# Gate and up projection: a fourth seven-product K pair per column chunk, and one weight sum made by an adding transfer

## The chip, the cores and the metric

The kernel runs on one core of one Trainium2 chip. The metric is the device time of one execution in microseconds. Before the change it was 2225.26 us, the median of three runs (2225.0 to 2226.5). A profiled execution is one further run, taken by the hardware profiler.

## The reference

Two layers of a residual trunk work on 256 tokens of width 2048 in float32. Only the feed-forward half of a layer bears on this case:

```python
def swiglu(h, w_gate, w_up, w_down):
    return (jax.nn.silu(h @ w_gate) * (h @ w_up)) @ w_down

for l in range(DEPTH):                       # DEPTH = 2
    h = rms_norm(x, pre_mix_norm[l])
    x = x + rms_norm(hybrid_mixer(h, l, ...), post_mix_norm[l])   # w_in 2048 x 6144, attention, w_o 2048 x 2048
    h = rms_norm(x, pre_ffn_norm[l])
    x = x + rms_norm(swiglu(h, w_gate[l], w_up[l], w_down[l]), post_ffn_norm[l])
```

w_gate and w_up are 2048 x 5632, w_down is 5632 x 2048. All weights are float32, and the result keeps float32's accuracy: every product is made of three matmuls on rounded halves of its operands.

## The kernel before, in words

**Weights as a stream.** All weight matrices are cut into pieces of 256 rows (a "K pair": two K tiles of 128) by 512 columns. `queue_pair` (L93) lists them in the order of use. `fetch` (L135) loads piece i with a DMA on SyncE's queue (L139) into a tile `raw`, of which there are four, each 128 x 2 x 512 float32 (512 KB). `feed` (L166) turns a piece into two tiles: `hi`, its rounded copy (ScalarE, L176), and `lo`, the rest (VectorE, L178); there are six of each. `weights` (L186) feeds four pieces ahead of the use (`LOOKAHEAD`). A load waits for a free `raw` tile, so for the end of an earlier piece's `lo`; a `hi` waits until TensorE has read an earlier piece's `hi`.

**Gate and up.** The 5632 columns are 11 chunks of 512 (loop at L827). A chunk has 8 K pairs, and for each K pair the stream holds a gate piece and then the up piece. There are two ways to multiply a K pair by the 256 tokens (two blocks of 128):

- `eight` (L810): 2 K tiles x 2 token blocks x 2 matrices are 8 products of 3 matmuls of 128x512 (L706 to L708), 24 in all. Both pieces are split as above.
- `seven` (L820): Strassen's scheme in Winograd's form over the 2 x 2 blocks (token block by K tile, K tile by gate or up), with 7 products, 21 matmuls, by `seven_products` (L723). It needs sums of token blocks (`pair_sums` and `token_sums`, made once per layer in the first chunk at the places that `FORM_AT` names) and sums of weight blocks: with g0, g1, u0, u1 for the two K tiles of the gate and up pieces, t1 = g0 + u0, t3 = u0 + u1, t2 = t1 + u1 and t4 = t2 + g1. Four of the products have no accumulator of their own in the output, so they gather in four further PSUM banks (p1, p6, p7, q5) over the chunk's seven-product pairs, and `shared_part` (L740) adds them up at the end.

`SEVEN` (L36) names the K pairs of a chunk that go by `seven`: 2, 4 and 6; the first chunk, which has its own order, has 4 and 6 (`FIRST_SEVEN`). `mixed_weights` (L144) makes the weight sums for such a pair: four additions on VectorE (L150, 128x512) from the two `raw` tiles into two tiles `T` of the pool `gu`, then the rounded copies `Th` (ScalarE, L159) and the rests `Tl` (VectorE, L161) of both, and the split of u1 alone (L154, L155).

At the end of a chunk VectorE adds up the shared parts (L744 to L747) and the results (L853 to L856) from PSUM, with ScalarE's Silu between; `flip` (L858) transposes them on TensorE (L862) during the next chunk.

**Down.** Two halves of 22 K pairs follow; six pairs of each go by seven products as well (`DOWN_SEVEN`, L40), with the same `mixed_weights`. The tiles `T`, `Th` and `Tl` then lie in a pool `sums`, which takes the space of the tokens' tiles `xF` once gate and up have read them (L868).

**Order.** A scheduler of the framework orders each engine's instructions when the program is built, and each engine then works through its queue strictly in that order. The tile pools hand a new tile the slot that is expected to come free first. The order of the loads on SyncE's queue and of the splits on VectorE's is thus fixed beforehand.

Of the kernel before, what the change touches and what calls it, by code (L numbers as in the profile page):

```python
# [17 lines left out]
P = 128  # L18
D = 2048
S = 256  # L20
L = 2
NT = S // P
KT = D // P
NH = 8
FF = 5632
CW = 512
# [16 lines left out]
LEVEL = 232  # L43


def lambda_init(layer):
    return 0.8 - 0.6 * math.exp(-0.3 * layer)


@with_exitstack  # L50
def kernel(
# [3 lines left out]
    w_in: bass.AP,  # L55
    w_o: bass.AP,
# [6 lines left out]
    w_gate: bass.AP,  # L63
    w_up: bass.AP,
    w_down: bass.AP,
    rope: bass.AP,
    x_columns: bass.AP,
    gain_columns: bass.AP,
    out: bass.AP,
# [21 lines left out]
    stream = []  # L91

    def queue_pair(w2d, kp, c):  # L93
        stream.append(
            w2d[kp * 2 * P : (kp + 1) * 2 * P, c * CW : (c + 1) * CW].rearrange("(k p) n -> p k n", p=P)
        )
        return len(stream) - 1

    plan = []
    sevens = set()  # L100
    for l in range(L):
        lay = {"in": {}, "o": {}, "gate": {}, "up": {}, "down": {}}
        chunks = []
        for g in range(2):
            chunks += [6 + g, 8 + g, 10 + g]
        for g in range(2):
            chunks += [g, 2 + g, 4 + g]
        lay["chunks"] = chunks
        for c in chunks:
            for kp in range(KT // 2):  # L110
                lay["in"][c, kp] = queue_pair(w_in[l], kp, c)
        order_o = [(c, kp) for kp in KP_O for c in (0, 1)]
        order_o += [(c, kp) for c in (2, 3) for kp in range(KT // 2)]
        lay["order_o"] = order_o
        for c, kp in order_o:
            lay["o"][c, kp] = queue_pair(w_o[l], kp, c)
        for c in range(FF // CW):
            for kp in FIRST_ORDER if c == 0 else range(KT // 2):
                lay["gate"][c, kp] = queue_pair(w_gate[l], kp, c)
                lay["up"][c, kp] = queue_pair(w_up[l], kp, c)  # L120
                if kp in (FIRST_SEVEN if c == 0 else SEVEN):
                    sevens.add(lay["up"][c, kp])
        for half in range(2):
            for kp in range(FF // P // 2):
                for c in (2 * half, 2 * half + 1):
                    lay["down"][c, kp] = queue_pair(w_down[l], kp, c)
                if kp in DOWN_SEVEN:
                    sevens.add(lay["down"][2 * half + 1, kp])
        plan.append(lay)
# [5 lines left out]
    def fetch(upto):  # L135
        while len(raws) < min(upto, len(stream)):
            i = len(raws)
            raw = wpool.tile([P, 2, CW], F32, tag="raw", bufs=4, name=f"raw{i}")
            loads.append(nc.sync.dma_start(raw, stream[i]))  # L139
            raws.append(raw)  # L140

    mix_pool = [None]

    def mixed_weights(i):  # L144

        g, u = raws[i - 1], raws[i]
        sums = [mix_pool[0].tile([P, 2, CW], F32, tag="T", bufs=2, name=f"T{i}_{j}") for j in range(2)]
        t1, t3, t2, t4 = sums[0][:, 0, :], sums[0][:, 1, :], sums[1][:, 0, :], sums[1][:, 1, :]
        for o, a, b in ((t1, g[:, 0, :], u[:, 0, :]), (t3, u[:, 0, :], u[:, 1, :]), (t2, t1, u[:, 1, :]), (t4, t2, g[:, 1, :])):
            nc.vector.tensor_tensor(out=o, in0=a, in1=b, op=ALU.add)  # L150
        parts = []
        hi = wpool.tile([P, 2, CW], F32R, tag="hi", bufs=6, name=f"hi{i}")
        lo = wpool.tile([P, 2, CW], F32R, tag="lo", bufs=6, name=f"lo{i}")
        nc.scalar.activation(hi[:, 1, :], u[:, 1, :], AF.Copy)  # L154
        nc.vector.tensor_tensor(out=lo[:, 1, :], in0=u[:, 1, :], in1=hi[:, 1, :].bitcast(F32), op=ALU.subtract)  # L155
        parts.append((hi[:, 1, :], lo[:, 1, :]))
        for j in range(2):
            th = mix_pool[0].tile([P, 2, CW], F32R, tag="Th", bufs=3, name=f"Th{i}_{j}")
            nc.scalar.activation(th, sums[j], AF.Copy)  # L159
            tl = mix_pool[0].tile([P, 2, CW], F32R, tag="Tl", bufs=3, name=f"Tl{i}_{j}")  # L160
            nc.vector.tensor_tensor(out=tl, in0=sums[j], in1=th.bitcast(F32), op=ALU.subtract)  # L161
            parts += [(th[:, k, :], tl[:, k, :]) for k in range(2)]
        b22, t1, t3, t2, t4 = parts
        return {"b22": b22, "t1": t1, "t2": t2, "t3": t3, "t4": t4}
# [50 lines left out]
    setup = tc.alloc_tile_pool(name="setup", bufs=1, side="right", reuse_waits="tile")  # L215
    idle = setup.tile([P, CW], BF16, name="idle")
# [10 lines left out]
    lams = setup.tile([P, 4, L * 64], F32, name="lams")  # L227
    negones = setup.tile([P, P], F32, name="negones")
# [6 lines left out]
    def late_constants():  # L235
# [16 lines left out]
        lprod = setup.tile([P, 2, L * 64], F32, name="lprod")  # L252
        lsum = setup.tile([P, 2, L], F32, name="lsum")
# [364 lines left out]
    def settle(pool, rs, evac):  # L618

        for t, h in ((0, 0), (0, 1), (1, 0), (1, 1)):  # L620
            load_x(t, h)
            yield 1
        late_constants()
        setup.release()
        rs += [inv_rms(t, pool, "in0") for t in range(NT)]
        yield 2
        scales(rs)
        evac()
# [121 lines left out]
    for l in range(L):  # L750
# [117 lines left out]
        mix_pool[0] = new_x_pool(f"sums{l}")  # L868
# [100 lines left out]
    "x", "w_in", "w_o", "lambda_q1", "lambda_k1", "lambda_q2", "lambda_k2",  # L969
    "post_mix_norm", "post_ffn_norm", "w_gate", "w_up", "w_down",  # L970
# [44 lines left out]
```

## Time and profile before

| what | value |
|---|---|
| median of the runs | 2225.26 us |
| the profiled execution | 2225.4 us |
| its span (first to last instruction) | 2223.6 us |
| mean granted TensorE clock | 0.998 |
| TensorE busy | 2205.6 us, 99% |
| VectorE busy | 1765.9 us, 79% |
| ScalarE busy | 1276.3 us, 57% |
| GpSimd busy | 37.4 us, 2% |
| DMA | 423.72 MB, 191 GB/s on average |

The profile names the engines PE (TensorE), PEld (its weight loads), DVE (VectorE), ACT (ScalarE), POOL (GpSimd) and SP (SyncE); SPq is SP's DMA queue. L176 is line 176 of the kernel. A row of a group reads: line, engine, operation, tiles written <- tiles read, shape, count, busy time and mean ns of one, idle time of the engine before them and what ended it. Consecutive matmuls overlap, so their spacing, not their length, is what one costs. A row of the timeline reads: start, length, engine, line, operation, tiles, and in brackets how long the engine had been idle and what released it.

### The profile page before, as it was taken

What the parts mean: (1) busy time and instruction counts of PE and PEld (TensorE: products, weight loads), DVE (VectorE), ACT (ScalarE), POOL (GpSimd) and SP (SyncE); (2) the same over time, 40 slices, a digit from 0 to 9 for tenths busy, and PEclk for the clock granted to TensorE, in tenths of its full rate; (3) what the DMA queues carried; (4) which work ended last, traced back from release to release, by engine and by line L of the source; (5) the groups of instructions that cost most, each with busy time, mean ns of one, the idle gap of its engine ahead of it and who ended that gap; (6) DMA issues with size and microseconds to landing.
All of it is one profiled execution on the core that took longest, in us unless ns stands there. A gap on an engine that the chain in (4) does not pass through costs nothing.

```text
span 2223.6 us, 28156 instructions
## 1 busy us (share of the span) xinstructions
PE 2205.6 (99%) x10117; PEld 1814.4 (82%) x10117; DVE 1765.9 (79%) x2505; ACT 1276.3 (57%) x1895; POOL 37.4 (2%) x76
## 2 busy tenths in 40 slices
PE   9999999999999999999999999999999999999998
PEld 7888888788888888888877888887888888888886
DVE  6666555899889989989876665558998898999897
ACT  6555554656555556656565455546655555566563
POOL 1100000000000000000010000000000000000000
PEclk9999999999999999999999999999999999999999
DMA  8655555466665665656555555554666565566564
GB/s 292 194 164 165 159 189 183 138 208 203 204 199 190 205 207 189 213 189 213 194 182 170 169 163 161 183 187 151 201 207 202 178 221 194 190 212 211 183 217 143
DMA packets 217996, 423.72 MB, mean 191 GB/s; under 512 B 13568, under 2 KB 14080, under 8 KB 217344
## 3 DMA queue, kind: packets, MB, share of 16 engines
q1 hardware_dynamic: 217712, 421.91, 58.8%
q8 instruction: 79, 1.29, 0.2%
q14 instruction: 61, 0.50, 0.1%
q10 hardware_dynamic: 144, 0.02, 0.0%
HBM read 419.77 MB, written 2.10 MB: 190 GB/s over the span
## 4 chain that ended last, share of the span: by engine, by line
PE 94%; ACT 2%; DVE 1%; DMA 1%; issue 0%; SPq 0%; DVEq 0%; ACTq 0%
PE c L707 10%; PE c L706 10%; PE c L708 10%; PE in L352 8%; PE in L354 8%; PE in L353 8%; PE dn L911 5%; PE dn L909 5%; PE dn L908 5%; PE o L354 2%; PE o L352 2%; PE o L353 2%; PE p L706 2%; PE p L707 2%; PE p L708 2%; ACT hi L176 1%
## 5 line engine op out<-in xcount | busy, mean ns | idle before, releaser
L178 DVE TENSOR_TENSOR lo<-raw,hi 128x1024 fp32r<-128x1024 f32 x695 | 843.9, 1224 | 309.6 <-ACT hi L176 304.4
L176 ACT ACTIVATE hi<-raw 128x1024 fp32r<-128x1024 f32 x695 | 726.9, 1056 | 497.8 <-PE in L354 164.9
L706 PE MATMUL c<-hi,xF 128*128 128x512 f32 x960 | 377.0, 394 | 1.4 <-ACT w L743 0.8
L707 PE MATMUL c<-lo,xF 128*128 128x512 f32 x960 | 373.9, 390 | 1.1 <-DVE lo L178 1.0
L708 PE MATMUL c<-hi,xF 128*128 128x512 f32 x960 | 374.0, 391 | 0.0
L159 ACT ACTIVATE Th<-T 128x1024 fp32r<-128x1024 f32 x176 | 185.7, 1056 | 141.7 <-DVE T L150 133.8
L161 DVE TENSOR_TENSOR Tl<-T,Th 128x1024 fp32r<-128x1024 f32 x176 | 214.2, 1217 | 4.4 <-ACT Th L159 3.8
L706 PEld LDWEIGHTS c<-hi,xF 128*128 128x128 f32 x960 | 180.5, 188 | 39.2 <-ACT w L743 1.2
L707 PEld LDWEIGHTS c<-lo,xF 128*128 128x128 f32 x960 | 180.6, 188 | 38.5 <-DVE lo L178 2.3
L708 PEld LDWEIGHTS c<-hi,xF 128*128 128x128 f32 x960 | 180.7, 188 | 37.8
L908 PE MATMUL dn<-hi,jh 128*128 128x512 f32 x464 | 180.7, 389 | 0.0
L909 PE MATMUL dn<-lo,jh 128*128 128x512 f32 x464 | 180.5, 389 | 0.0
L352 PE MATMUL in<-hi,xI 128*128 128x512 f32 x384 | 154.0, 401 | 0.4 <-ACT xI L293 0.4
L352 PE MATMUL in<-hi,xT 128*128 128x512 f32 x384 | 153.8, 401 | 0.5 <-ACT hi L176 0.5
L354 PE MATMUL in<-hi,xI 128*128 128x512 f32 x384 | 150.3, 391 | 0.3 <-DVE xI L298 0.3
L353 PE MATMUL in<-lo,xI 128*128 128x512 f32 x384 | 150.0, 391 | 0.5 <-DVE lo L178 0.5
L353 PE MATMUL in<-lo,xT 128*128 128x512 f32 x384 | 149.8, 390 | 0.5 <-DVE lo L178 0.5
L354 PE MATMUL in<-hi,xT 128*128 128x512 f32 x384 | 150.1, 391 | 0.0
L911 PE MATMUL dn<-hi,jl 128*128 128x512 f32 x464 | 142.8, 389 | 0.0
L150 DVE TENSOR_TENSOR T<-T,raw 128x512 f32<-128x512 f32 x176 | 120.5, 684 | 1.2
L911 PEld LDWEIGHTS dn<-hi,jl 128*128 128x128 f32 x464 | 87.1, 188 | 18.1
L908 PEld LDWEIGHTS dn<-hi,jh 128*128 128x128 f32 x464 | 87.1, 188 | 18.1
(295 smaller groups left out, 3513.8 us busy)
## 6 DMA issues: line engine op xcount, KB each, us to landing
raw<-in_w_in_dram SPq DMA_DIRECT2D x191, 512.0 KB, 3.8
raw<-in_w_gate_dram SPq DMA_DIRECT2D x176, 512.0 KB, 3.8
raw<-in_w_up_dram SPq DMA_DIRECT2D x176, 512.0 KB, 4.5
raw<-in_w_down_dram SPq DMA_DIRECT2D x176, 512.0 KB, 4.5
raw<-in_w_o_dram SPq DMA_DIRECT2D x64, 512.0 KB, 4.0
xr<-in_x_columns_dram SPq DMA_DIRECT2D x8, 256.0 KB, 6.9
x<-in_x_dram SPq DMA_DIRECT2D x4, 512.0 KB, 8.6
gpost_mix<-in_post_mix_norm_dram SPq DMA_DIRECT2D x2, 1024.0 KB, 6.9
```

Of the source, the lines that this page charges most:

```text
L161: nc.vector.tensor_tensor(out=tl, in0=sums[j], in1=th.bitcast(F32), op=ALU.subtract)
L176: nc.scalar.activation(hi, raw, AF.Copy)
L178: nc.vector.tensor_tensor(out=lo, in0=raw, in1=hi.bitcast(F32), op=ALU.subtract)
L352: nc.tensor.matmul(a, sh, hi[:, kk, :], start=first and kk == 0, stop=False)
L353: nc.tensor.matmul(a, sh, lo[:, kk, :], start=False, stop=False)
L354: nc.tensor.matmul(a, sl, hi[:, kk, :], start=False, stop=last and kk == 1)
L706: nc.tensor.matmul(a, sh, hi, start=first, stop=False)
L707: nc.tensor.matmul(a, sh, lo, start=False, stop=False)
L708: nc.tensor.matmul(a, sl, hi, start=False, stop=last)
L908: nc.tensor.matmul(accs[c, t], sh, hi[:, kk, :], start=first, stop=False)
L909: nc.tensor.matmul(accs[c, t], sh, lo[:, kk, :], start=False, stop=False)
L911: nc.tensor.matmul(accs[c, t], sl, hi[:, kk, :], start=False, stop=last)
```

## The change

1. `SEVEN` becomes (2, 4, 5, 6): in chunks 1 to 10 of each layer K pair 5 goes by seven products too. `FORM_AT` gets an entry for its token sums, made in the first chunk.
2. The sums of weight blocks are made in another way. The up piece of a seven-product pair is no longer loaded into a `raw` tile but into a tile `T` of its own (`summed`), and a second DMA, on GpSimd's queue, adds the gate piece's first half onto the tile's first half: T = (t1, u1). `fetch` issues both up to `EARLY` = 4 stream places ahead of the piece's turn. `mixed_weights` splits T as one 128x1024 tile, then makes t2 = t1 + u1 in T's second half, and t3 = t2 - g0 and t4 = t2 + g1 in place of the gate piece in its `raw` tile: three VectorE additions where there were four, and splits of 1024, 512 and 1024 columns where there were 512, 1024 and 1024. `Th` and `Tl` become two tiles of 128 x 3 x 512 instead of three of 128 x 2 x 512; there are three tiles `T` in gate and up and two in down.
3. The weights come to the device in the order of the stream, as one tensor in which each piece is a contiguous 512 KB and each of its 128 rows 4 KB (`weights_laid_out`); before, a row of a piece was two runs of 2 KB in the weight matrix.
4. To make room, the pool `setup` is gone (its tiles use `lo` and `t2` slots), the feed-forward pool has five `t2` tiles instead of six, and the loads in the last output-projection pieces run at most 12 places ahead of that stage's first such piece instead of up to 15.

```diff
-SEVEN = (2, 4, 6)
+SEVEN = (2, 4, 5, 6)
-FORM_AT = {1: 4, 3: 6, 5: 2}
+FORM_AT = {1: 4, 3: 6, 4: 5, 5: 2}
+EARLY = 4
...
+    stream = [weights_in_turn[i].rearrange("p (k n) -> p k n", k=2) for i in range(len(order))]
...
     def fetch(upto):
         while len(raws) < min(upto, len(stream)):
             i = len(raws)
+            for j in range(i, min(i + EARLY + 1, mix_pool[2])):
+                if j in sevens and j not in sums:
+                    summed(j)
+            if i in sevens:
+                raws.append(sums[i])
+                continue
             raw = wpool.tile([P, 2, CW], F32, tag="raw", bufs=4, name=f"raw{i}")
             loads.append(nc.sync.dma_start(raw, stream[i]))
             raws.append(raw)
+    sums = {}
+    def summed(i):
+        sums[i] = mix_pool[0].tile([P, 2, CW], F32, tag="T", bufs=mix_pool[1], name=f"T{i}")
+        loads.append(nc.sync.dma_start(sums[i], stream[i]))
+        nc.gpsimd.dma_start(sums[i][:, 0, :], stream[i - 1][:, 0, :], accum_op=ALU.add)
...
     def mixed_weights(i):
         g, u = raws[i - 1], raws[i]
-        sums = [mix_pool[0].tile([P, 2, CW], F32, tag="T", bufs=2, name=f"T{i}_{j}") for j in range(2)]
-        t1, t3, t2, t4 = sums[0][:, 0, :], sums[0][:, 1, :], sums[1][:, 0, :], sums[1][:, 1, :]
-        for o, a, b in ((t1, g[:, 0, :], u[:, 0, :]), (t3, u[:, 0, :], u[:, 1, :]), (t2, t1, u[:, 1, :]), (t4, t2, g[:, 1, :])):
-            nc.vector.tensor_tensor(out=o, in0=a, in1=b, op=ALU.add)
...
+        th = mix_pool[0].tile([P, 3, CW], F32R, tag="Th", bufs=2, name=f"Th{i}")
+        tl = mix_pool[0].tile([P, 3, CW], F32R, tag="Tl", bufs=2, name=f"Tl{i}")
+        def split(h, l, w):
+            nc.scalar.activation(h, w, AF.Copy)
+            nc.vector.tensor_tensor(out=l, in0=w, in1=h.bitcast(F32), op=ALU.subtract)
+        split(hi, lo, u)
+        t2 = u[:, 1, :]
+        nc.vector.tensor_tensor(out=t2, in0=u[:, 0, :], in1=t2, op=ALU.add)
+        nc.vector.tensor_tensor(out=g[:, 0, :], in0=t2, in1=g[:, 0, :], op=ALU.subtract)
+        nc.vector.tensor_tensor(out=g[:, 1, :], in0=t2, in1=g[:, 1, :], op=ALU.add)
+        split(th[:, 2, :], tl[:, 2, :], t2)
+        split(th[:, 0:2, :], tl[:, 0:2, :], g)
...
-                fetch(idx + 8 + kp)
+                fetch(min(idx + 8 + kp, idx + 12))
...
-        pool = tc.alloc_tile_pool(name=f"ffn{l}", bufs=6, reuse_waits="tile")
+        pool = tc.alloc_tile_pool(name=f"ffn{l}", bufs=5, reuse_waits="tile")
...
-        mix_pool[0] = gu
+        mix_pool[:] = gu, 3, plan[l]["down"][0, 0]
...
-        mix_pool[0] = new_x_pool(f"sums{l}")
+        mix_pool[:] = new_x_pool(f"sums{l}"), 2, plan[l]["down"][3, FF // P // 2 - 1] + 1
```

More of the change, by code (lines that the diff above doesn't have):

```diff
@@ L43, with weight_order, queue_pair, weights_laid_out @@
 LEVEL = 232
+EARLY = 4
 def lambda_init(layer):
     return 0.8 - 0.6 * math.exp(-0.3 * layer)
+def weight_order():
+    order = []
+    def queue_pair(name, l, kp, c):
+        order.append((name, l, kp, c))
+        return len(order) - 1
+    plan = []
+    sevens = set()
+    for l in range(L):
+        lay = {"in": {}, "o": {}, "gate": {}, "up": {}, "down": {}}
+        chunks = []
+        for g in range(2):
+            chunks += [6 + g, 8 + g, 10 + g]
+        for g in range(2):
+            chunks += [g, 2 + g, 4 + g]
+        lay["chunks"] = chunks
+        for c in chunks:
+            for kp in range(KT // 2):
+                lay["in"][c, kp] = queue_pair("w_in", l, kp, c)
+        order_o = [(c, kp) for kp in KP_O for c in (0, 1)]
+        order_o += [(c, kp) for c in (2, 3) for kp in range(KT // 2)]
+        lay["order_o"] = order_o
+        for c, kp in order_o:
+            lay["o"][c, kp] = queue_pair("w_o", l, kp, c)
+        for c in range(FF // CW):
+            for kp in FIRST_ORDER if c == 0 else range(KT // 2):
+                lay["gate"][c, kp] = queue_pair("w_gate", l, kp, c)
+                lay["up"][c, kp] = queue_pair("w_up", l, kp, c)
+                if kp in (FIRST_SEVEN if c == 0 else SEVEN):
+                    sevens.add(lay["up"][c, kp])
+        for half in range(2):
+            for kp in range(FF // P // 2):
+                for c in (2 * half, 2 * half + 1):
+                    lay["down"][c, kp] = queue_pair("w_down", l, kp, c)
+                if kp in DOWN_SEVEN:
+                    sevens.add(lay["down"][2 * half + 1, kp])
+        plan.append(lay)
+    return order, plan, sevens
+def weights_laid_out(inputs):
+    import numpy as np
+    order = weight_order()[0]
+    out = np.empty((len(order), P, 2 * CW), np.float32)
+    for o, (name, l, kp, c) in zip(out, order):
+        w = inputs[name][l, kp * 2 * P : (kp + 1) * 2 * P, c * CW : (c + 1) * CW]
+        o[...] = w.reshape(2, P, CW).transpose(1, 0, 2).reshape(P, 2 * CW)
+    return out
 @with_exitstack
@@ L68 @@
     gain_columns: bass.AP,
+    weights_in_turn: bass.AP,
     out: bass.AP,
@@ L88, in four_banks @@
         return [make(n) for make, n in zip(makers, names)]
[L91 to L129, printed above, removed]
+    order, plan, sevens = weight_order()
+    stream = [weights_in_turn[i].rearrange("p (k n) -> p k n", k=2) for i in range(len(order))]
     ready = {}
```

41 lines of the change are left out of this document (13 added, 28 removed).

## The prediction, made before the changed kernel ran

> **What bounds the kernel now.** I read the page first, then the busy time of each engine in the stretch of full gate-and-up chunks, then the timelines of TensorE and VectorE there, and last the two seams of that stretch.
>
> ```profile
> span 2223.6 us, 28156 instructions
> PE 2205.6 (99%) x10117; PEld 1814.4 (82%) x10117; DVE 1765.9 (79%) x2505; ACT 1276.3 (57%) x1895; POOL 37.4 (2%) x76
> PE 94%; ACT 2%; DVE 1%; DMA 1%; issue 0%; SPq 0%; DVEq 0%; ACTq 0%
> ```
> ```profile
> 470.00:895.00 425.00, 425.00 (x1916) 352.08 (x1915) 381.90 (x455) 241.73 (x280) 0.00 (x0) 1.00 0.62 202
> ```
> ```profile
> 659.80 0.39 PE L707 MATMUL c<-lo,xF 128*128 128x512 f32 x1
> ...
> 667.96 0.39 PE L707 MATMUL c<-lo,xF 128*128 128x512 f32 x1
> ```
> ```profile
> L743 ACT COPY w<-p x11: 566/568/569, 443.3 to 868.4; 128x512 f32<-128x512 f32 x11
> ```
>
> TensorE's matmuls bound it: 99% busy, 94% of the chain of waits, and in the stretch of layer 0's chunks and the start of down (columns: window, length, PE, PEld, DVE, ACT, POOL, clock, DMA share, GB/s) 425.00 of 425.00 us at clock 1.00. VectorE is close behind, at 381.90 of 425, so 10% idle. The two matmul rows are the first and last of 37 without a gap: (667.96 - 659.80) / 36 = 0.2267 us each. L743 runs once per chunk, so the ten chunks that follow the first take (868.4 - 443.3) / 10 = 42.5 us each. That is 5 x 24 + 3 x 21 = 183 matmuls = 41.5, and the transposes of the last chunk:
>
> ```profile
> 882.68 0.87 PE actT_ps L862 x8
> ```
>
> **Part 1: fewer matmuls.** Pair 5 goes from 24 to 21 matmuls in 10 chunks of 2 layers: 60 x 0.2267 = **13.6 us less**. A chunk would take 42.5 - 0.7 = 41.8 us. This counts in full only if VectorE and the loads keep up.
>
> **Part 2: VectorE's load per chunk.** Rows of its queue at work without pause:
>
> ```profile
> 626.48 0.68 DVE L150 TENSOR_TENSOR T<-T,raw 128x512 f32<-128x512 f32 x1
> 627.09 0.68 DVE L155 TENSOR_TENSOR lo<-raw,hi 128x512 fp32r<-128x512 f32 x1
> 627.69 0.68 DVE L150 TENSOR_TENSOR T<-T,raw 128x512 f32<-128x512 f32 x1
> 628.29 1.22 DVE L161 TENSOR_TENSOR Tl<-T,Th 128x1024 fp32r<-128x1024 f32 x1
> 629.42 1.22 DVE L178 TENSOR_TENSOR lo<-raw,hi 128x1024 fp32r<-128x1024 f32 x1
> 630.56 1.22 DVE L161 TENSOR_TENSOR Tl<-T,Th 128x1024 fp32r<-128x1024 f32 x1
> ```
>
> From start to start a 128x512 operation costs 0.60 us and a 128x1024 one 1.135. An ordinary pair is two large ones, 2.27. A seven-product pair was 1.135 (gate's lo) + 4 x 0.60 + 0.60 + 2 x 1.135 = 6.4, and becomes 1.135 + 1.135 + 3 x 0.60 + 0.60 + 1.135 = 5.8. With ten operations at the chunk's end (L744 to L747, L853, L855, L856; about 6.2) a chunk was 5 x 2.27 + 3 x 6.4 + 6.2 = 36.8 and becomes 4 x 2.27 + 4 x 5.8 + 6.2 = 38.5. VectorE does 1.7 us more in 0.7 us less. Its real idle time was 10% of 42.5 = 4.3 us, so it falls to about 1.9: 95% busy. It isn't the bound by sum; by order it might be.
>
> **Part 3: the longest chain.** I took the changed program's order of instructions on each engine, with what each waits for, and walked one chunk; zero is TensorE's start on pair 0. Pairs then start at 5.9, 11.75, 16.5, 21.95, 26.7, 31.5 and 36.2 (24 or 21 matmuls each, the transposes behind pair 0). `hi` of pair 3's gate waits until pair 0's gate was last read, at 21 x 0.2267 = 4.8. One ScalarE copy then takes
>
> ```profile
> L176 ACT ACTIVATE hi<-raw 128x1024 fp32r<-128x1024 f32 x695 | 726.9, 1056 | 497.8 <-PE in L354 164.9
> ```
>
> 1.06, and VectorE, which had been waiting with pair 2's sums queued behind this `lo`, comes to the end of pair 2's `Tl` at about 12.1. They are due at pair 2's eleventh matmul, 14.0. From there it has no pause until pair 6's `Tl`: nine `lo`, three large and three small `Tl`, nine additions, 12 x 1.135 + 12 x 0.60 = 20.8, so 33.0. They are due at pair 6's thirteenth matmul, 31.5 + 2.7 = 34.2. So the chunk's slack is about 1.2 us, less the semaphore gaps that my spacings leave out (in before, 42.5 - 36.8 = 5.7 of idle by spacings, but 4.3 measured: 1.4 us in a chunk, some 0.8 in this stretch). I charge 0.1 us per chunk: **+2 us** over 20 chunks; from below 0, from above 0.5 per chunk, +10.
>
> **Part 4: the loads.** The adding transfer isn't in the trace. The nearest rows by size (KB, us from issue to landing):
>
> ```profile
> raw<-in_w_up_dram SPq DMA_DIRECT2D x176, 512.0 KB, 4.5
> raw<-in_w_down_dram SPq DMA_DIRECT2D x176, 512.0 KB, 4.5
> ...
> out_dram<-x SPq DMA_DIRECT2D x8, 256.0 KB, 2.3
> ...
> gains<-in_gain_columns_dram SPq DMA_DIRECT2D x1, 32.0 KB, 9.4
> ```
>
> It moves 256 KB but must also read the tile, so I take it as a 512 KB load, 4.5 us; bounds 2.3 and 9.4. The Trainium skill ("DMA: Bandwidth & Descriptors", section "Anatomy of one DMA — SWDGE (gpsimd) path") gives 2.0 us plus bytes / 436e3 for a transfer issued from GpSimd: an estimate of 2.6 us here. No run yet shows one; by it, the +3.3 below would be 0.
>
> In full chunks most tiles `T` are asked for 20 us ahead, since VectorE frees them then. The tight one is pair 6's: its slot comes free at 11.0 (pair 2's t2 is split), its load lands at 15.5, the sum at 20.1, and `hi` wants it at 22.3: 2.2 us to spare. At 9.4 it would be 2.7 late, which uses up the slack of part 3 and costs about 2 us per chunk. The extra bytes are 4 x 0.26 MB on 8.4 MB per chunk, twice that with the reads of the tile, at a DMA share of 0.62: room is there. Rows of 4 KB instead of 2 KB: I take nothing; from zero to 2 us less in the opening, where loads are awaited.
>
> **Part 5: the first chunk.** Here TensorE does wait in before:
>
> ```profile
> 430.00:440.00 10.00, 8.63 (x30) 6.61 (x31) 10.00 (x17) 4.72 (x6) 0.00 (x0) 0.83 0.47 124
> ```
> ```profile
> 411.01 0.37 SPq L139 DMA_DIRECT2D raw<-in_w_up_dram  x1
> 419.26 0.37 SPq L139 DMA_DIRECT2D raw<-in_w_gate_dram  x1
> ```
> ```profile
> 453.90 0.50 PE L706 MATMUL c<-hi,xF 128*128 128x512 f32 x1 [0.23 <-DVE w L745]
> ```
>
> 30 matmuls where 44 fit. Loads stood still for 8 us, because a fifth piece needs a free `raw` tile. In the changed order pair 4's and pair 6's up pieces go to `T` right behind the load at 411.0, since their space is free by then. VectorE's queue in before:
>
> ```profile
> 422.07 1.22 DVE L178 TENSOR_TENSOR lo<-raw,hi 128x1024 fp32r<-128x1024 f32 x1
> 429.42 1.22 DVE L161 TENSOR_TENSOR Tl<-T,Th 128x1024 fp32r<-128x1024 f32 x1
> 430.55 0.42 DVE L807 TENSOR_TENSOR f<-xF 128x256 f32<-128x256 f32 x1
> 430.89 0.28 DVE L715 TENSOR_TENSOR s<-f 128x128 f32<-128x128 f32 x1
> 431.09 0.28 DVE L713 TENSOR_TENSOR s<-f 128x128 f32<-128x128 f32 x1
> 441.60 1.22 DVE L161 TENSOR_TENSOR Tl<-T,Th 128x1024 fp32r<-128x1024 f32 x1 [1.33 <-ACT Th L159]
> ```
>
> Walking the changed queue on from the `lo` at 422.1: five f at 0.34 and seven s at 0.20, which now stand ahead, then four large and five small splits and additions (4 x 1.135 + 5 x 0.60 = 7.5) end pair 4's large `Tl` at 422.1 + 1.1 + 3.1 + 7.5 = 433.8, against 430.6 in before. Four large (4.5) and six small (3.6) operations further on, pair 6's ends at 441.9, where before ended at 442.8. So the second chunk starts at about 433.8 + 80 x 0.2267 = 451.9 (the 80 matmuls from there to the chunk's end), where it started at 453.9. That is 2 us less in layer 0; layer 1 has a smaller hole. Together **-2 us** (between -4 and +4).
>
> **Part 6: the first seven-product pair of down.** `T` now lies where the tokens' tiles lay, and SP can ask for it only when the last gate-and-up matmul has read them; before, the raw pieces were there long ahead and VectorE's additions were all that waited.
>
> ```profile
> 877.87 0.69 DVE L855 TENSOR_TENSOR w<-c,w 128x512 f32<-128x512 f32 x1
> ...
> 882.28 0.68 DVE L150 TENSOR_TENSOR T<-raw,raw 128x512 f32<-128x512 f32 x1
> ```
>
> Zero is that matmul's end, about 877.1. The load lands at 4.9 (4.5 after its issue, with a little for the queue), the sum at 9.4, `hi` at 10.5; then VectorE works through four `lo`, three additions and both `Tl`: 5 x 1.135 + 4 x 0.60 = 8.1, to 18.6. The pair starts at 11.75, and in the changed order, where parts of the next pair are put between, the last-needed matmul is its 24th: due at 11.75 + 23 x 0.2267 = 17.0. The stall is 1.6 us per layer: **+3.3 us**; at 2.3 per add nothing, at 9.4 it is 6.5 per layer, 13 in all. Behind the waiting `lo` stand the next pairs' splits in VectorE's queue, for which TensorE has work until then.
>
> **The rest.** Token sums for pair 5 (2.1 us of VectorE per layer) lie in the first chunk and are in part 5. SP's queue: loads of `T` stand ahead of raw loads, but each waits for an event no later than the raw load behind it. In down, pairs lie 15 us apart and VectorE gets 0.6 us less each: nothing. The opening's moved tiles: nothing.
>
> **The sum.** -13.6 + 2 - 2 + 3.3 = -10.3 us. On the profiled execution of 2225.4 (span 2223.6 and 1.8 around it, 0.1 above the median) that is 2215.
>
> **The rivals.**
>
> - *A: the vector queue becomes the bound.* If the stretch of part 3 takes longer than its slack, each us costs 20 us, since the next chunk's chain starts from TensorE's pair 0. The likeliest cause is a load that lands late: pair 5's gate piece is asked for when pair 3's `lo` ends (7.0) and wanted at 13, and with the loads of `T` and the adds beside it 6 us may not do. For it speaks 95% load, three seven-product pairs in a row and queues that can't overtake; against it that before ran at full rate with VectorE at 90%. It is slower than before when the stall passes 0.6 us per chunk. At 1.3 us: 20 x 1.2 more than my sum, 2239.
> - *B: slow adds.* At 9 us each, down's starts cost 12 instead of 3.3: 2224, no change.
> - *C: GpSimd is kept from issuing the adds while VectorE works.* Then pair 6's sum waits for the next pause, at about 33 instead of 20: 10 us later than wanted, 20 times: about 2400. The trace has nothing for it: the busy POOL time lies outside this stretch (0.00 above). The Trainium skill ("SBUF — State Buffer", section "Who interferes with whom") says that a VectorE instruction with two SBUF inputs holds up only GpSimd instructions that read SBUF, and infers that descriptor generation is not held up by it; no run yet shows that.
> - *D: the seams gain more.* Contiguous loads land sooner, and parts 3 and 6 cost nothing: -13.6 - 4 - 2: 2206.
> - *E: T is not loaded ahead.* In the first chunk and in full chunks the changed order shows it ahead; where it isn't is part 6.
>
> **How the numbers follow.** Forecast 0.52 (own range 2208 to 2220), A 0.22, B 0.12, C 0.04, D 0.10. Forecast and D are faster by over 0.2% (4.5 us, about what a measurement of this kernel can tell from no change): 0.62. B is within: 0.12. A and C are slower: 0.26. The range reaches from D's end, 2204, over most of A to 2240; C and A's far end stay out.
>
> **What would show it.** TensorE at 100% in full chunks and L743's line every 41.8 us: parts 1 to 3. A wait of TensorE for a `Tl` in pair 2 or 6 of each chunk: A. An add that takes about 4.5 us from issue to landing; over 9, B. A hole of one or two us near the start of down: part 6. The second chunk about 2 us sooner behind the last output projection: part 5. The sum is wrong above all if VectorE's operations get longer than 0.60 and 1.135, since the slack is only 1.2 us in 42.

## The result: 0.5% slower, and the profile after

The changed kernel takes 2235.98 us, the median of five runs (2234.4 to 2240.0), against 2225.26 before: a ratio of 1.0052, 95% interval 1.0037 to 1.0067. The forecast was 2215, in its own range 2208 to 2220. The profiled execution is the slowest of the five (2240.0), so the table below also gives e7, whose edit touches only the opening and whose profiled execution lies near the median.

The page of the changed kernel, for the lines of the page that the prediction shows of before:

```profile
span 2237.9 us, 28440 instructions
...
PE 2200.9 (98%) x10057; PEld 1802.2 (81%) x10057; DVE 1789.1 (80%) x2531; ACT 1309.5 (59%) x1937; POOL 132.0 (6%) x184
...
PE 71%; DVE 13%; DMA 6%; issue 4%; ACT 4%; POOL 0%; DVEq 0%; ACTq 0%; SPq 0%; POOLq 0%
```

The 60 matmuls are gone (10057 of 10117). But TensorE no longer makes 94% of the chain of waits, only 71%; VectorE and DMA have 19% of it. The busy times in the stretch of full chunks, columns as before, and the line that runs once per chunk (L770 now):

```profile
470.00:895.00 425.00, 418.12 (x1862) 341.91 (x1861) 392.08 (x473) 251.99 (x294) 33.91 (x39) 1.00 0.71 221
```
```profile
L770 ACT COPY w<-p x11: 563/567/570, 445.7 to 872.3; 128x512 f32<-128x512 f32 x11
```

TensorE has 6.9 us of holes where it had none, and ten chunks take 426.6 us where they took 425.1, with 30 matmuls fewer. What TensorE, VectorE and ScalarE waited for between 460 and 870 us (total us, times, longest):

```profile
PE p L733 <- ACT Th L181: 2.8, 3, 1.5
PE p L734 <- DVE Tl L182: 2.4, 4, 0.9
```
```profile
DVE lo L207 <- ACT hi L205: 27.4, 24, 2.8
```
```profile
ACT hi L205 <- DMA raw<-in_weights_in_turn_dram: 44.6, 31, 4.4
...
ACT hi L181 <- DMA T<-in_weights_in_turn_dram: 0.9, 1, 0.9
```

TensorE waits for the split sums `Th` and `Tl`, five times of seven in pair 6. ScalarE's split waits for a raw load, VectorE's `lo` waits for that split, and everything behind both stands still. For an adding transfer (last row) a split waited once, for 0.9 us. The loads in the same stretch (KB, median us to landing; POOLq is the adding transfer):

```profile
raw<-in_weights_in_turn_dram SPq DMA_DIRECT2D x115, 512.0 KB, 5.0
T<-in_weights_in_turn_dram SPq DMA_DIRECT2D x37, 512.0 KB, 4.6
T<-in_weights_in_turn_dram POOLq DMA_DIRECT2D x37, 256.0 KB, 6.1
```

The add takes 6.1 us here (6.5 over the whole run), not 4.5. VectorE's operations did not get longer (1.22 and 0.68 us, as in the rows before), although GpSimd issued an add every 11 us (0.87 us each).

In which stage the time came, from TensorE's first matmul of each stage in the profiled executions (us; median of the runs in the last column). The stages left out take the same time before and after, to 0.1 us; what follows the last matmul takes 0.8 us more:

| kernel | opening, layer 0 | gate-up, 0 | down, 0 | gate-up, 1 | down, 1 | median |
|---|---|---|---|---|---|---|
| before | 300.1 | 474.7 | 233.1 | 472.7 | 231.9 | 2225.3 |
| after | 301.8 | 477.2 | 237.4 | 474.5 | 234.9 | 2236.0 |
| e7 constants' pool back | 299.6 | 473.5 | 238.6 | 473.9 | 234.4 | 2233.1 |
| e2 no adding transfer | 304.3 | 465.6 | 234.1 | 465.7 | 232.7 | 2214.9 |
| e3 eights resident | 303.9 | 466.8 | 236.3 | 466.7 | 234.3 | 2221.3 |
| e5 adds elsewhere | 302.1 | 482.7 | 233.8 | 480.1 | 233.1 | 2248.9 |
| e6 tiny adds | 303.0 | 467.8 | 237.2 | 466.5 | 233.1 | 2220.0 |
| e1 three pairs | 303.7 | 473.1 | 240.0 | 472.4 | 236.1 | 2232.9 |
| e4 rows alone | 300.7 | 471.6 | 233.0 | 471.5 | 231.9 | 2222.4 |
| e12 VectorE's sums | 299.1 | 470.5 | 241.2 | 471.4 | 240.0 | 2235.7 |
| e14 e13, last chunk three | 300.1 | 470.0 | 234.3 | 472.2 | 234.1 | 2220.6 |
| e16 fourth pair, old sums, last chunk three | 299.5 | 469.5 | 233.0 | 468.7 | 231.9 | 2217.3 |

The forecast wanted gate and up 13.6 us shorter in both layers together; they are 4.4 us longer. Down was to lose 3.3 and lost 7.3; the opening was to lose nothing and lost 1.7. Two seams show how. TensorE at the first seven-product pair of down, and the ScalarE and VectorE rows that led to it:

```profile
899.02 0.82 PE L733 MATMUL p_d<-Th,sh 128*128 128x512 f32 x2 [2.35 <-ACT Th L181]
```
```profile
891.48 1.06 ACT L181 ACTIVATE hi<-T 128x1024 fp32r<-128x1024 f32 x1 [2.82 <-DMA T<-in_weights_in_turn_dram]
```
```profile
892.57 1.23 DVE L182 TENSOR_TENSOR lo<-T,hi 128x1024 fp32r<-128x1024 f32 x1 [2.45 <-ACT hi L181]
```
```profile
895.00:905.00 10.00, 7.65 (x27) 0.83 0.82 272
```

`hi` waits for the add, VectorE for `hi`, and TensorE has a hole of 2.35 us. The ten microseconds around it (last row, PE alone: length, busy, clock, DMA share, GB/s) hold 27 matmuls where 45 stand in an undisturbed ten: 18 x 0.2267 = 4.1 us, so 1.7 more than the hole, since the granted clock fell behind it (0.83 on average over the ten). Layer 1 has the like, a hole of 2.52 us. In the opening TensorE waited for GpSimd's rotation of the first heads (first row: total, times, longest, up to 306 us), which began at 47.89 in place of 40.83 us, held by ScalarE's scales (second row after, third before):

```profile
PE qkT_ps L707 <- POOL tok L601: 2.3, 2, 1.8
```
```profile
47.89 0.74 POOL L598 TENSOR_TENSOR ra<-tok,rope_sb 128x128 f32<-128x128 f32 x1 [10.35 <-ACT rs_in L305]
```
```profile
40.83 0.46 POOL L570 TENSOR_TENSOR ra<-tok,rope_sb 128x128 f32<-128x128 f32 x1 [38.48 <-ACT tok L671]
```

### The profile page after: what moved, and what is told of

It reads as the page before. It is cut to its first block, busy times and chain, and to the rows that moved or that the text cites. A ratio compares the mean times of both kernels' runs of the same rounds, so it can differ in the third digit from the quotient of the medians.

```text
span 2237.9 us, 28440 instructions
## 1 busy us (share of the span) xinstructions
PE 2200.9 (98%) x10057; PEld 1802.2 (81%) x10057; DVE 1789.1 (80%) x2531; ACT 1309.5 (59%) x1937; POOL 132.0 (6%) x184
## 3 DMA queue, kind: packets, MB, share of 16 engines
q1 hardware_dynamic: 117488, 421.91, 55.2%
## 4 chain that ended last, share of the span: by engine, by line
PE 71%; DVE 13%; DMA 6%; issue 4%; ACT 4%; POOL 0%; DVEq 0%; ACTq 0%; SPq 0%; POOLq 0%
PE in L380 7%; PE in L382 7%; PE in L381 7%; DMA raw<-in_weights_in_turn_dram 5%; PE c L733 5%; PE c L734 5%; PE c L735 5%; PE dn L938 5%; PE dn L936 5%; PE dn L935 4%; DVE lo L207 3%; DVE Tl L182 2%; PE o L382 2%; PE o L381 2%; PE o L380 2%
## 5 line engine op out<-in xcount | busy, mean ns | idle before, releaser
L207 DVE TENSOR_TENSOR lo<-raw,hi 128x1024 fp32r<-128x1024 f32 x675 | 824.1, 1225 | 311.4 <-ACT hi L205 307.3
L733 PE MATMUL c<-hi,xF 128*128 128x512 f32 x820 | 321.0, 395 | 2.4 <-DVE w L774 1.3
L735 PE MATMUL c<-hi,xF 128*128 128x512 f32 x820 | 318.8, 391 | 0.0
L734 PE MATMUL c<-lo,xF 128*128 128x512 f32 x820 | 318.7, 389 | 0.0
L168 POOL DMA_DIRECT2D T<-in_weights_in_turn_dram x108 | 94.1, 871 | 1754.1 <-DMA T<-in_weights_in_turn_dram 821.8
L733 PEld LDWEIGHTS c<-hi,xF 128*128 128x128 f32 x820 | 154.0, 188 | 35.3 <-DVE w L774 2.5
L735 PEld LDWEIGHTS c<-hi,xF 128*128 128x128 f32 x820 | 153.9, 188 | 32.3
L734 PEld LDWEIGHTS c<-lo,xF 128*128 128x128 f32 x820 | 154.1, 188 | 30.9
L182 DVE TENSOR_TENSOR Tl<-raw,Th 128x1024 fp32r<-128x1024 f32 x108 | 131.5, 1217 | 8.7 <-ACT Th L181 8.7
L181 ACT ACTIVATE Th<-raw 128x1024 fp32r<-128x1024 f32 x108 | 113.8, 1053 | 37.9 <-DVE raw L188 37.8
L182 DVE TENSOR_TENSOR lo<-T,hi 128x1024 fp32r<-128x1024 f32 x108 | 131.4, 1216 | 4.4 <-ACT hi L181 4.4
L181 ACT ACTIVATE Th<-T 128x512 fp32r<-128x512 f32 x108 | 67.9, 629 | 112.1 <-DVE T L186 96.3
```

Source lines behind the costliest of these rows:

```text
L182: nc.vector.tensor_tensor(out=l, in0=w, in1=h.bitcast(F32), op=ALU.subtract)
L207: nc.vector.tensor_tensor(out=lo, in0=raw, in1=hi.bitcast(F32), op=ALU.subtract)
L733: nc.tensor.matmul(a, sh, hi, start=first, stop=False)
L734: nc.tensor.matmul(a, sh, lo, start=False, stop=False)
L735: nc.tensor.matmul(a, sl, hi, start=False, stop=last)
```

## Experiments

Three theories stood at the start. **V**: VectorE's in-order queue, 92 to 95% full with four pairs, is late by itself. **L**: the raw loads land late. **A**: the adding transfers are the cause.

### Which part: e1 to e4

e1: `SEVEN = (2, 4, 6)` and `FORM_AT = {1: 4, 3: 6, 5: 2}` in the changed kernel.

> The changed kernel with three seven-product pairs (2, 4, 6) per chunk as before, and everything else of the change kept: the sum order, the adding transfer, tiles loaded ahead, 4 KB rows. If the fourth pair's own VectorE and load work makes the stalls (theories V and L), the chunks run at 42.4 us without stalls as in the kernel before, so 13.6 us more matmul time and 20 to 24 us less stall than the changed kernel: about 2226 to 2229. If the adding transfers make the stalls wherever they stand (theory A), three of them per chunk still stall: 0.9 us a chunk over 42.4, so about 2245.

Measured: 2232.93 us, ratio to before 1.0031 (1.0019 to 1.0042). Chunks run at 42.4 us without stalls from the third on, and the adds land in 4.6 us; so neither the new sums nor the adds stall a chunk that has room. In the profiled execution, the slowest of its six, the rest lies in the opening (1.9 us above the changed kernel's) and in down (2.6 and 1.2 above), whose code is the changed kernel's.

e2: one line less.

```diff
-        nc.gpsimd.dma_start(sums[i][:, 0, :], stream[i - 1][:, 0, :], accum_op=ALU.add)
```

> The changed kernel without the adding transfer: the tile T holds only the up or right-hand weights, so the sum t1 misses one of its two terms and the output is not the reference's. Theory A (adds land at 6 to 6.5 us and are what ACT's first split waits for): chunk period 41.8 us without stalls and no hole at the start of down, about 2236 - 20 to 24 - 6 = 2206 to 2210. Theories L and V (raw loads late, or VectorE's queue): the stalls of 1.0 to 1.2 us a chunk stay, only the hole of 2.35 us at the start of each down may shrink: 2229 to 2236.

Measured: **2214.89 us**, ratio 0.9947 (0.9934 to 0.9959), 21 us below the changed kernel. Its stretch from 470 to 895 us, and its waits between 460 and 870:

```profile
470.00:895.00 425.00, 423.87 (x1903) 348.58 (x1902) 402.57 (x482) 258.45 (x302) 0.00 (x0) 1.00 0.58 204
```
```profile
ACT hi L204 <- DMA raw<-in_weights_in_turn_dram: 37.3, 28, 3.0
```
```profile
DVE lo L206 <- ACT hi L204: 19.2, 24, 1.5
```

The same VectorE work, now 402.57 of 425 us busy, and TensorE runs on: from the fifth on, layer 0's chunks come every 41.8 us. Theory V falls. The longest waits for a load went from 4.4 to 3.0 us, and of VectorE for `hi` from 2.8 to 1.5.

e3: the eight-product pairs of chunks 1 to 10 read x in place of loads.

```diff
+            if i in light:
+                raws.append(xs[i % 2][:, 0 : 2 * CW].rearrange("p (k n) -> p k n", k=2))
+                continue
             raw = wpool.tile([P, 2, CW], F32, tag="raw", bufs=4, name=f"raw{i}")
```

> The changed kernel, with the eight-product pairs of chunks 1 to 10 of gate and up reading their weights from the resident x tiles in place of loads, so that half of that stage's weight transfers are gone and no split of those pairs can wait for a load; the output is not the reference's. Matmuls, VectorE and ScalarE instructions are the same in number and shape. Theory L (late loads): chunk period 41.4 to 41.8 us, stalls under 0.2 us a chunk, about 2236 - 20 = 2216. Theory V (VectorE is 92 to 95 % busy and its in-order queue is late even with its data there): the stalls of 1.0 to 1.2 us a chunk stay, 2231 to 2236.

Measured: 2221.27 us, ratio 0.9980 (0.9971 to 0.9989); chunks of 41.8 us, as L has it, and the rest above its 2216 in the opening and in down. All adds are still there. With half of the other loads gone they land sooner too:

```profile
raw<-in_weights_in_turn_dram SPq DMA_DIRECT2D x44, 512.0 KB, 3.4
T<-in_weights_in_turn_dram SPq DMA_DIRECT2D x37, 512.0 KB, 3.2
T<-in_weights_in_turn_dram POOLq DMA_DIRECT2D x37, 256.0 KB, 3.9
```

So the stalls need both, the adds and the full loads: either taken away, they go. That leaves two ways: the adds land late for the one who waits for them, or their bytes make the other loads late.

e4: the kernel before, with `weights_laid_out` and nothing else of the change.

> The kernel before, with one part of the change alone: the weights lie in the order of use, so each partition's row of a transfer is 4 KB in one piece in place of two of 2 KB. Sums, pools and pairs as before. If only the first loads gain by it, as the prediction had it: 2223 to 2226, the first matmul at most 1 us sooner, and the first weight-bound stage no longer. If the longer rows shorten every raw load, the gate-up stage of the kernel before (42.4 us a chunk) does not change, since its TensorE has no holes there. If the 1.7 us that the opening stage lost comes from the row layout, it shows here as 308 in place of 306.5 us at the end of that stage.

Measured: 2222.37 us, ratio 0.9987 (0.9978 to 0.9996). The opening is no longer (300.7), and full chunks take 42.4 us as expected; gate and up of layer 0 gain 3.2 us, all before the fourth chunk. The prediction's "nothing" was wrong by 3.6 us at the median (0.9 to 4.9 by the interval); its bound was 2.

### Waiting or bytes: e5 and e6

e5 sends each add elsewhere, e6 shrinks it:

```diff
-        nc.gpsimd.dma_start(sums[i][:, 0, :], stream[i - 1][:, 0, :], accum_op=ALU.add)
+        nc.gpsimd.dma_start(xs[i // 2 % 2][:, 0:CW], stream[i - 1][:, 0, :], accum_op=ALU.add)     # e5
+        nc.gpsimd.dma_start(sums[i][:, 0, 0:8], stream[i - 1][:, 0, 0:8], accum_op=ALU.add)        # e6
```

> The changed kernel with each adding transfer sent into the resident x tiles in place of T: the same number and size of transfers, but no split waits for one, and none waits for T's load; t1 misses one term and x is spoilt, so the output is not the reference's. Theory wait (the add's landing 6.1 us behind T's is the late link): as without the adding transfer, 2213 to 2218, chunks at 41.8 us. Theory traffic (the adds' 28 MB, at twice the transfer-engine time per byte, delay the raw loads of the same moments, 5.0 in place of 4.5 us): the stalls stay, 2230 to 2236.

> The changed kernel with adding transfers of 8 of 512 columns, in the same places and with the same waits; t1 misses most of one term, so the output is not the reference's. Theory traffic: without the bytes it runs as without the adding transfer, 2213 to 2218. Theory wait, if the add's 6.1 us are mostly fixed cost (issue, descriptors, completion): the tiny add lands at 4 us or more and stalls stay, 2225 to 2236; if they are mostly bytes, it lands at 2 to 3 us and the time is also 2213 to 2220, which then leaves the run beside this one to tell wait from traffic.

Measured: e5 2248.87 us, ratio 1.0103 (1.0090 to 1.0117); e6 2219.98, 0.9972 (0.9962 to 0.9982). e5's adds did not keep their times. They no longer wait for a tile `T`, only for the add before them into the same x tile, so GpSimd issued all 54 of layer 0, down's twelve among them, between 410 and 645 us: about twice as densely as the changed kernel, and none behind. e5 while its adds run, and after that:

```profile
470.00:645.00 175.00, 167.44 (x734) 134.70 (x733) 158.56 (x189) 99.96 (x116) 30.04 (x36) 0.99 0.85 245
645.00:885.00 240.00, 240.00 (x1079) 198.12 (x1078) 224.51 (x263) 145.83 (x170) 0.87 (x1) 1.00 0.58 202
```

In the first of these stretches TensorE is busy 167.44 of 175 us with 36 adds, in the changed kernel 170.56 with 17, in e2 174.54 with none; in the second, without adds, it has no hole. e6's loads and adds, 460 to 870 us:

```profile
raw<-in_weights_in_turn_dram SPq DMA_DIRECT2D x119, 512.0 KB, 4.5
T<-in_weights_in_turn_dram SPq DMA_DIRECT2D x37, 512.0 KB, 4.0
...
T<-in_weights_in_turn_dram POOLq DMA_DIRECT2D x37, 4.0 KB, 4.1
```

In gate and up it is the bytes. Where no split waits for an add, the stalls stay as long as the adds run (e5), and where every sum waits for a tiny one they are nearly gone (467.8 and 466.5 us, against 465.6 and 465.7 without any). Since tiny adds also land 2 us sooner, e6 alone would not tell the two apart; e5 does, and so does the single wait of 0.9 us for an add in the changed kernel. In down it is the wait, in layer 0 at least: a tiny add leaves a hole of 2.12 us there and 237.2 us, where e2 takes 234.1. In layer 1 the tiny add costs 0.4 us, and why is open. e5 has no adds left in down, so its 233.8 and 233.1 only repeat e2. Even 4 KB land only after 4.1 us.

### Other ways to make the sum, other places: e7 to e12

e7 undoes the move of the opening's constants: `setup` is again a pool of its own for `idle`, `lams`, `negones`, `lprod` and `lsum`.

> The changed kernel with the opening's constants back in a pool of their own (as before), in place of the shared slots t2. If those slots hold GpSimd up behind the x squares, and so the first rotate that a TensorE transpose waits for (the hole of 2.3 us at 50 us): the first stage ends at 306 to 307 in place of 308 to 310 us, and the whole is 2 to 3.5 us shorter, 2232.5 to 2234. If the hole comes from something else (the added GpSimd work of the change is not in this stage), nothing changes: 2236.

Measured: 2233.13 us, 1.0031 (1.0020 to 1.0043), 2.9 us below the changed kernel; the hole is gone. The profiled executions agree: in the six kernels with the moved tiles (the changed one, e1, e2, e3, e5, e6) the opening ends 308.2 to 309.9 us behind the span's start, in all others at 305.7 to 306.5.

e8, on top of e7, takes the adding transfer out and puts into `mixed_weights`:

```diff
+        nc.gpsimd.tensor_tensor(out=u[:, 0, :], in0=u[:, 0, :], in1=g[:, 0, :], op=ALU.add)
         split(hi, lo, u)
```

> The changed kernel with t1 = T + gate weights made by a GpSimd tensor_tensor of 128x512 in place of the adding transfer, and the constants' pool of e7. Nothing is left out. GpSimd's 128x128 additions of this trace take 0.46 to 1.51 us; four times that is 1.8 to 6 us. At 2 us it comes beside the split of the gate weights and hides: as without the adding transfer less 2 to 3 us of e7, 2211 to 2215. At 5 us or more, or if it slows VectorE's operations (1.22 us for 128x1024 now) by 5 % or more, the stalls come back: 2230 or more.

Measured: 2279.62 us, 1.0244 (1.0230 to 1.0258). Groups between 460 and 870 us:

```profile
L183 POOL TENSOR_TENSOR T<-T,raw 128x512 f32<-128x512 f32 x38 | 74.6, 1966 | 342.4 <-DMA raw<-in_weights_in_turn_dram 320.3 <-DVE Tl L181 9.6 <-DVE lo L181 3.5
...
L186 DVE TENSOR_TENSOR T<-T 128x512 f32<-128x512 f32 x37 | 31.9, 863 | 0.2
```

The sum takes the hoped-for 2 us, yet it cost the most. It can begin only when the gate piece is there, where the adding transfer needed only T; and VectorE's addition t2 went from 0.684 to 0.863 us on average, t3 and t4 from 0.685 to 0.742. The Trainium skill ("SBUF — State Buffer", section "Who interferes with whom") says that a VectorE instruction with two SBUF inputs contends with a GpSimd instruction that reads SBUF; this trace agrees. How the 46 us above e7 divide between the late start and the slower additions was not measured.

e9 is e7 with `DOWN_SEVEN = (3, 5, 8, ...)`.

> e7 (constants in a pool of their own), and the first seven-product pair of down moved from pair 2 to pair 3, 5.4 us of matmuls later. If the hole at the start of down (2.35 us and about 1.9 us of halved clock behind it) is the wait for the first sum tile, whose slot comes free only when gate and up end: it goes, down takes 233.5 to 235 in place of 238.6 and 234.4 us, and the whole is 2226 to 2229. If VectorE's or ScalarE's own queue is late there, the hole moves to pair 3 with most of its size: 2231 to 2234.

Measured: 2233.33 us, 1.0029 (1.0018 to 1.0040): nothing gained, as the second theory's figure has it. The first row is ScalarE's, the second VectorE's:

```profile
888.07 1.06 ACT L181 ACTIVATE hi<-T 128x1024 fp32r<-128x1024 f32 x1 [6.12 <-DMA T<-in_weights_in_turn_dram]
```
```profile
889.16 1.23 DVE L182 TENSOR_TENSOR lo<-T,hi 128x1024 fp32r<-128x1024 f32 x1 [5.25 <-ACT hi L181]
```

ScalarE stood 6.12 us in front of a sum that was needed one pair later, with other pairs' splits behind it. VectorE, too, stood waiting and was not late by its own work. So a later use of the sum alone did not help: the wait kept its place in ScalarE's queue. That a later place in the queue would help was not tried.

e10 is e9 with seven-product pairs at 1, 3, 5 and 6.

> e9, with the seven-product pairs of gate and up at 1, 3, 5 and 6 in place of 2, 4, 5 and 6 (first chunk: 5 and 6, with pair 4 between them), the same number of products, sums and transfers. If the adding transfers hurt because three tiles of sums and their adds stand together, spacing them takes most of the stalls of chunks 2 to 4 away: 2215 to 2222. If the bytes hurt wherever they lie, or VectorE's backlog behind a chunk's end is what they meet (which pair 1 meets sooner): as e9 or slower, 2226 to 2240.

Measured: 2262.75 us, 1.0170 (1.0153 to 1.0188), against the first theory and beyond the second's range. TensorE's waits from 400 to 875 us name the chunk's end:

```profile
PE actT_ps L891 <- DVE w L885: 13.9, 15, 2.3
```

With pair 1's sums in VectorE's queue beside the last chunk's results (L885), TensorE's transposes wait for those results; that the sums hold them up is read from the order, not tested.

e11 and e12, on top of e9, let VectorE make t1, in pairs 2 and 6 or everywhere.

```diff
+        if i in by_vector:
+            nc.vector.tensor_tensor(out=u[:, 0, :], in0=u[:, 0, :], in1=g[:, 0, :], op=ALU.add)
         split(hi, lo, u)
```

> e9, with t1 of pairs 2 and 6 of chunks 1 to 10 made by VectorE (0.69 us each) and only pairs 4 and 5 by an adding transfer. Traffic theory: half of the adding bytes gone, at least half of the gate-up stalls (8 us a layer) gone, VectorE at 95 + 3 % of the chunk still keeps up: 2217 to 2223. If VectorE's queue has no room for 1.4 us more a chunk: stalls stay or grow, 2228 or more.

> e9, with all t1 made by VectorE and no adding transfer at all; T is still loaded ahead. Without the adds and without more VectorE work the chunks ran at 41.8 us with VectorE busy 388.6 of 410 us; four more operations of 0.69 us a chunk make it 415 of 410, so VectorE becomes the bound at about 42.4 to 43 us a chunk: 2222 to 2236 in all, near the kernel before. If the in-order queue with no slack costs more: 2240 or more. If VectorE's operations overlap enough to keep 41.8: 2210 to 2215.

Measured: e11 2254.12 us, 1.0124 (1.0110 to 1.0138), against the traffic theory; e12 2235.68, 1.0042 (1.0029 to 1.0055). VectorE's waits for T's `hi` in e11, then in e12, 460 to 870 us:

```profile
DVE lo L184 <- ACT hi L183: 27.5, 19, 2.7
```
```profile
DVE lo L184 <- ACT hi L183: 5.2, 10, 0.5
```

In e11 the program's order puts `lo` right behind the addition whose `hi` it needs, so VectorE idles for ScalarE's copy, 19 times; in e12 other work stands between. e12's stretch, and ten microseconds at its seam to down:

```profile
460.00:870.00 410.00, 407.44 (x1819) 333.60 (x1818) 400.39 (x489) 246.90 (x285) 0.00 (x0) 1.00 0.59 195
872.00:882.00 10.00, 6.48 (x20) 4.09 (x20) 10.00 (x15) 7.59 (x10) 0.00 (x0) 0.73 0.96 387
```

VectorE is 98% busy and TensorE still at 407 of 410. Against e2, gate and up take 4.9 and 5.7 us more, down 7.1 and 7.3: most is lost at the seam, with 20 matmuls in ten microseconds.

### The fourth pair alone, and the seam: e13 to e16

e13 is e12 with `DOWN_SEVEN` as it was. e14 is e13 with `LAST_SEVEN = (2, 4, 5)` for the last chunk of each layer. e15 is e4 with `SEVEN = (2, 4, 5, 6)`, its `FORM_AT` and `bufs=5` in the feed-forward pool: the kernel before's sums. e16 is e15 with that `LAST_SEVEN`.

> e12 (all t1 by VectorE, no adding transfers) with the first seven-product pair of down back at pair 2. If moving that pair cost the 7 to 8 us a layer of down in e12: down 233 to 235 us, about 2222 in all. If VectorE's backlog at the end of the last chunk costs them (TensorE had 3.5 us of holes and halved clock at 872 to 882): no change, 2234 to 2238.

> e13 with three seven-product pairs (2, 4, 5) in the last chunk of each layer in place of four: 0.7 us more of matmuls, about 4 us less of VectorE work there a layer, and the shared part one pair sooner. Backlog theory: the 6 us lost at the seam go, 11 us for both layers: 2222 to 2227. If the moved pair was it, as e13 plus 1.4 us.

> One part alone: the kernel before with its weights in the order of use (e4, 2222.4), and the fourth seven-product pair (5) with the sums made as before, by four VectorE operations; the shared slots t2 are five in place of six for room. VectorE's work per chunk is that of e12, 98 % of 41.8 us. If the gain of 13.6 us of matmuls is kept but for e12's stalls and its seam: 2220 to 2226. If the sums' tiles (two slots, made late, not loaded ahead) cannot keep up with three seven-product pairs in a row: 2235 or more. If VectorE has room enough: 2209 to 2214.

> e15 with three seven-product pairs (2, 4, 5) in each layer's last chunk. Backlog theory: the seam's 6 us a layer less 0.7 us: 8 to 11 us faster than e15. If e15 has no hole at the seam: 1 to 2 us slower than e15.

Measured: e13 2235.56 us, 1.0046 (1.0033 to 1.0058); e14 2220.61, 0.9980 (0.9972 to 0.9989); e15 2222.56, 0.9989 (0.9980 to 0.9998); **e16 2217.29, 0.9964 (0.9951 to 0.9976)**, the fastest that computes everything, and faster than both kernels. The moved pair cost nothing; taking VectorE work out of the last chunk won 15 us in e13 and 5 in e15, so its backlog at the end of gate and up cost at least that. (The shared parts also end one pair sooner there; the runs do not tell the two apart.) e16's stretch and seam:

```profile
460.00:870.00 410.00, 408.22 (x1827) 335.54 (x1826) 403.83 (x495) 255.15 (x286) 0.00 (x0) 1.00 0.58 206
870.00:880.00 10.00, 10.00 (x50) 8.36 (x49) 10.00 (x15) 8.14 (x11) 0.00 (x0) 1.00 0.41 142
```

## Why the prediction was wrong, step by step

**Part 1 was right.** Undisturbed chunks take 41.8 us (e2, e3, and the last ones of the changed kernel).

**Part 2 was right, its worry too large.** VectorE at 95% (402.57 of 425) held TensorE back by at most 1.1 of 425 us in e2, and at 98% by 2.6 of 410 in e12 and 1.8 in e16. A busy VectorE cost little in these runs as long as its queue seldom waited.

**Part 4 failed: "room is there".** It weighed the adds' bytes against a mean DMA share of 0.62, and took the add as late only for its own reader. Not its reader but the raw loads of the same moments became late, in the median from 4.5 to 5.0 us and in the longest wait from 3.0 to 4.4 (e2 against the changed kernel), and these loads stand on part 3's chain. The add itself took 6.1 us, not 4.5, yet a split waited for it only once in full chunks.

**Part 3's charge failed with it.** 0.1 us per chunk was charged; gate and up lost 20.4 us to e2 in the profiled execution, 16.1 in e7's, so 0.8 to 1.0 us per chunk. That is rival A with the cause it named, a load that lands late beside the adds, and with its sign, TensorE's waits for `Th` and `Tl`, though not in each chunk; its price of 2239 for 1.3 us per chunk was near the 2236 measured. The slack of 1.2 us had been worked out, but not set against how much a load's landing spreads, and so A got 0.22 only.

**Part 5: right in sum, not in cause.** The first 186 matmuls of gate and up, the first chunk's number, took 49.8 us before and 46.8 after in layer 0, 48.2 and 47.4 in layer 1. With the 4 KB rows alone (e4) they took 47.3 and 47.1: the rows bring nearly all of it.

**Part 6: right mechanism, too small.** The hole is 2.35 us, not 1.6, and the lower clock behind it costs about 1.7 more; down lost 7.3, not 3.3. Without adds (e2) 5.5 of the 7.3 are gone, and a tiny add keeps the hole in layer 0 (e6), so the wait for the add is its cause there.

**"The opening's moved tiles: nothing" was wrong**, by 2 to 3 us (e7: 2.9 at the median, 2.2 in the profiled opening).

**Rivals B to E.** B's adds of 9 us did not come: the slowest took 8.6. C did not happen: VectorE was busy 92% of the stretch and the adds' issue took 0.87 us each beside it, as the Trainium skill ("SBUF — State Buffer", section "Who interferes with whom") infers for descriptor generation. D's contiguous loads did gain (e4), its seams did not. E did not apply: in full chunks a split waited once for a `T`.

In sum: the changed kernel without the bytes and waits of its adds is 2214.9, the forecast's 2215, in part by luck, since the rows' gain of 3.6 us and the opening's loss of 2.9 are both in it and neither in the forecast. The adds cost 21.1: 5.1 for waits and issue (e6 less e2) and 16.0 for bytes, the later landing that the bytes bring included. What stays open: why the stalls of one execution lie in chunks 2 to 4 alone (e7) and of another in later chunks too (after), and whether adds timed into the quiet stretches of each chunk would be free, which was not tried; e5's ran in fewer microseconds, not in quieter ones.

## What to carry to other kernels

An idle transfer path is not free room: where loads are on a chain with a microsecond of slack, added bytes must be weighed against the burst they fall into, not against the mean share. Test a transfer's price by sending it where nobody waits and by shrinking it to a few bytes; the two together tell its bytes from its wait, if you look when the transfers then run: freed of its wait, one can come much earlier and denser. And a nearly full in-order engine cost little here until something in its queue waited, so look at the waits, and at the end of a stage, where its backlog comes due.

## What the runs showed of the hardware beyond that

- **Bytes of an adding transfer cost about twice as much transfer-engine time.** Over the whole run of the changed kernel (queue, packets, MB, share of 16 engines):

```profile
q1 hardware_dynamic: 117488, 421.91, 55.2%
q0 software_dynamic: 15552, 28.32, 7.6%
```

That is 0.131% per MB for plain loads and 0.268% for adds. Shorter rows (2 KB in place of 4) are not the reason: the kernel before loaded the same 421.91 MB in 2 KB rows at 58.8%, 0.139% per MB.
- **An add of 4 KB took 4.1 us from issue to landing, of 256 KB 3.9 to 6.3 (medians between 460 and 870 us)**, the least with the DMA share at 0.43 (e3), the most at 0.70 (e7). The Trainium skill ("DMA: Bandwidth & Descriptors", section "Anatomy of one DMA — SWDGE (gpsimd) path") gives 2.0 us plus bytes / 436e3, an estimate of 2.6 us for 256 KB; no add here came near it in the median.
- **Behind short holes TensorE's clock was halved.** Two holes, of 1.46 and 0.94 us, and the stretches behind them (TensorE alone: length, busy, clock, DMA share, GB/s):

```profile
702.96 0.51 PE L733 MATMUL p<-Th,sh 128*128 128x512 f32 x1 [1.46 <-ACT Th L181]
704.41 0.50 PE L734 MATMUL p<-Tl,sh 128*128 128x512 f32 x1 [0.94 <-DVE Tl L182]
...
706.26 0.63 PE L733 MATMUL c<-hi,sh 128*128 128x512 f32 x1
706.68 0.63 PE L734 MATMUL c<-lo,sh 128*128 128x512 f32 x1
```
```profile
704.00:706.00 2.00, 1.59 (x5) 0.74 1.10 291
706.00:708.00 2.00, 2.00 (x7) 0.50 1.03 334
```

Matmuls then come 0.42 us apart instead of 0.2267. The Trainium skill ("TensorE: Matmul & The Clock Gate", section "Part 1: The HAM clock gate (the "warmup" mystery)") gives half rate after an idle window of about 3.4 us; the half rate agrees, but 2.4 us of holes were enough here, and at the start of down a single one of 2.35.
